# RMSNorm in a hybrid decoder: squares of four channel chunks summed in fp32 before the ones-matmul

## The chip, the cores and the metric

The kernel runs on all 8 cores of one Trainium2 chip, the same program on each (data parallel: one prompt sequence and 16 sample sequences per core). The metric is the device time of the slowest core, in microseconds. Most executions of one kernel agree within 0.3%. In some executions the cores of one die show a lower granted clock and the time is some per cent longer ("slow"); only fast executions are compared here, or, where a chip never was fast, the cores of its undisturbed die (a die is cores 0 to 3, or 4 to 7).

Five engines matter: TensorE (PE, matmuls, writes PSUM), VectorE (DVE), ScalarE (ACT), GpSimd (POOL) and SyncE (SP, DMA). Tiles lie in SBUF, the memory on the chip; the sums of the matmuls lie in PSUM. Each engine executes its own list of instructions in order. Here these lists are fixed when the program is built, by a list scheduler inside the kernel that works with modelled durations.

## The reference, cut to what matters

```python
def _rmsnorm(x, g):
    x32 = x.astype(jnp.float32)
    y = x32 * lax.rsqrt(jnp.mean(x32 * x32, axis=-1, keepdims=True) + RMS_EPS)
    return (y * g.astype(jnp.float32)).astype(x.dtype)

# per layer (2 layers), D_MODEL = 1024
hn = _rmsnorm(x, norm_in);  z = hn @ w_in          # 8 blocks of 1024 columns
...                                                # gated conv, RG-LRU, two output products, merge
x = x + merged @ w_o
gate = sigmoid(_rmsnorm(x, norm_pe) @ w_pg)
x = x + (p @ w_pe) * gate
# at the end: y = _rmsnorm(x, norm_final)
```

There are five norms per token: two per layer and a final one.

## The kernel before

Activations lie feature-major: a token tile of `n` = 424 (or 416) tokens is 8 chunks of 128 channels by `n` tokens. There are 5 token tiles, in two groups, so 25 norms of a tile. The mean over channels crosses partitions, so it is done by TensorE: the square of each chunk is the moving operand against a 128x128 tile that holds 1/1024 ("ones"), and the 8 products accumulate in one PSUM bank.

```python
def norm(t, xs, gcol, prio, final=False, split=(), yield_=0.0):
    n = TN[t]
    hv = [Val("buf", f"hn{t}.{i}") for i in range(KC // 2)]     # bf16 result, two chunks each
    bk = Val("bank", "nps")
    for k in range(KC):                                         # KC = 8 squares, bf16
        ...
        G.op([("act", d_act(n)), ("pool", d_ptt(n)), ("dve", d_stt(n))],   # any of three engines
             fsq, [xs[k]], [(h, p)], prio)
    for k in range(KC):                                         # 8 ones-matmuls
        G.op([("pe", d_mm(n, 1))], lambda e, en, h=h, a=a, k=k: e.matmul(
            out=ps(bk, 0, n), lhsT=ones[:], rhs=b16(h, a, a + n), start=(k == 0), stop=(k == KC - 1)),
            [(h, p), st_ones], [bk], prio, gate=True)
    ...                                                         # rstd = exp(-0.5 ln(mean + eps)) on ScalarE
    for k in range(KC):                                         # hn = x * g * rstd, mostly on VectorE (L570)
        ...
```

`G.op` gives the scheduler the engines that may take an operation, with a modelled duration for each. The scheduler places every operation on the engine that would end it first, by these numbers:

```python
def d_stt(n):  return 0.075 + 1.04e-3 * n    # VectorE tensor_tensor:         0.52 us at 424
def d_sttp(n): return 0.13 + 1.04e-3 * n     # ... with a scalar per partition: 0.57 us
def d_ptt(n):  return 0.3 + 2.4e-3 * n       # GpSimd tensor_tensor:          1.32 us
def d_mm(n, k=8): return k * (n + 6) / 2400. # TensorE, k matmuls:            0.179 us each
```

Two streams of work are interleaved to keep TensorE full: the "A" phase of one token group and the "B" phase of another (output products, merge, `w_o`, second norm, gate). In the A phase a channel block's convolution result is cast to bf16 (L668, ScalarE or VectorE) and goes through two 128x128 gate matmuls (L732, L735).

Of the kernel before, what the change touches and what calls it, by code (L numbers as in the profile page):

```python
# [7 lines left out]
AF = mybir.ActivationFunctionType  # L8
ALU = mybir.AluOpType

D = 1024
KC = 8
# [11 lines left out]
TN = (424, 424, 424, 424, 416)  # L24
T0 = tuple(sum(TN[:i]) for i in range(len(TN)))
GROUPS = ((0, 1), (2, 3, 4))
BUFE = 428
NBUF = 82
RA_N, RA_E = 6, 2048
# [38 lines left out]

class Op:
    __slots__ = ("engs", "fn", "R", "W", "prio", "aset", "dma", "npred", "succ", "ready", "idx", "vals",  # L70
                 "alloc", "eng", "start", "fin", "gate", "stream", "done", "look")


class Graph:
# [17 lines left out]
        self.ops = []  # L92
        self.stream = 0

    def op(self, engs, fn, R, W, prio, aset=None, dma=None, gate=False, after=()):
        o = Op()
        o.engs, o.fn, o.prio, o.aset, o.dma, o.gate = engs, fn, prio, aset, dma, gate
        o.R = [(r if isinstance(r, tuple) else (r, None)) for r in R]
        o.W = [(w if isinstance(w, tuple) else (w, None)) for w in W]
        o.idx = len(self.ops)  # L100
        o.look = self.WIN if dma is None else self.WIN_W if dma[0] in ("d_ra", "d_rb") else 0.0
        if prio < 0:
            o.look = 1e9
        o.stream, o.done = self.stream, False
        o.succ = []
        o.ready = 0.0
        preds = set(after)

        def parts(v, p):
            return (0, 1) if p is None else (p,)  # L110

        for v, p in o.R:
            for q in parts(v, p):
                w = v.lastw.get(q)
                if w is not None:
                    preds.add(w)
                v.readers.setdefault(q, []).append(o)
        for v, p in o.W:
            for q in parts(v, p):
                for r in v.readers.get(q, ()):  # L120
                    if r is not o:
                        preds.add(r)
                w = v.lastw.get(q)
                if w is not None:
                    preds.add(w)
                v.lastw[q] = o
                v.readers[q] = []
        o.vals = {id(v): v for v, _ in o.R + o.W}
        o.alloc = []
        for v in o.vals.values():  # L130
            if v.kind != "static":
                if not v.ops:
                    o.alloc.append(v)
                v.ops.append(o)
        o.npred = len(preds)
        for q in preds:
            q.succ.append(o)
        self.ops.append(o)
        return o

    def schedule(self):
# [55 lines left out]
        while n_left:  # L197
            best = None
            for e in ENG:
                T = free[e]  # L200
                eb = None
                for o in cand[e]:
                    if o.prio < 1e6 and (o.prio > head[o.stream] + o.look or o.prio > head[0] + self.WIN_B):
                        continue
                    a = avail(o) if o.alloc else 0.0
                    if a is None:
                        continue
                    s0 = s = max(T, o.ready + (self.MARGIN if e == "pe" and o.prio > 0 else 0.0), a)
                    key = o.prio
                    if e == "act" and o.aset and not cur[0] & self.SETS[o.aset]:  # L210
                        s = max(T + SW, o.ready, a)
                        key += 30.0
                    if len(o.engs) > 1:

                        d = dict(o.engs)[e]
                        if any(x != e and max(free[x], o.ready, a) + dx < s + d - 0.05 for x, dx in o.engs):
                            continue
                    k2 = (s0 > T + 0.02, s0 if s0 > T + 0.02 else 0.0, key, o.idx)
                    if eb is None or k2 < eb[0]:
                        eb = (k2, s, o)  # L220
                if eb is not None and (best is None or eb[1] < best[0]):
                    best = (eb[1], e, eb[2])
            if best is None:
                stuck = [(e, o.idx, [v.name for v in o.alloc]) for e in ENG for o in cand[e]]
                raise RuntimeError(f"stuck: {stuck[:20]} free {len(bufs['buf'])} {len(bufs['bank'])}")
            s, e, o = best
            dur = dict(o.engs)[e]
            if e == "act" and o.aset:
                cur[0] = (cur[0] & self.SETS[o.aset]) or self.SETS[o.aset]
            for v in o.alloc:  # L230
                if v.kind in ringn:
                    v.phys = v.seq % ringn[v.kind]
                else:
                    fl = bufs[v.kind]
                    x = min(fl)
                    fl.remove(x)
                    v.phys = x[1]
            o.eng, o.start, o.done = e, s, True
            advance(o.stream)
            free[e] = s + dur  # L240
            if o.dma is not None:
                st = max(dma_free[0], s + dur)
                dma_free[0] = st + o.dma[1]
                o.fin = dma_free[0] + (2.4 if e == "pool" else 1.7)
            else:
                o.fin = s + dur + self.LAT[e]["dve"]
            for x, _ in o.engs:
                cand[x].remove(o)
            for q in o.succ:
                q.npred -= 1  # L250
                q.ready = max(q.ready, (s + dur if q.dma is not None and q.dma[0] == o.dma[0] and o.dma[0] in ("d_ra", "d_rb") else o.fin)
                              if o.dma is not None else s + dur + self.LAT[e][q.engs[0][0]])
                if q.npred == 0:
                    for x, _ in q.engs:
                        cand[x].append(q)
            for v in o.vals.values():
                if v.kind == "static":
                    continue
                v.left -= 1
                v.free_at = max(v.free_at, o.fin)  # L260
                if v.left == 0:
                    if v.kind in ringn:
                        ringfree[v.kind][v.seq] = v.free_at
                    else:
                        bufs[v.kind].append((v.free_at, v.phys))
            order.append(o)
            n_left -= 1
# [72 lines left out]
def build_nc():  # L340
# [25 lines left out]
    G = Graph()  # L366
    from contextlib import ExitStack
    with ExitStack() as ctx:
# [16 lines left out]
        ones = sb("ones", [128, 128], BF16)  # L385
# [12 lines left out]
        def f32(v, a, b):  # L398
            return arena[v.phys][:, a:b]

        def b16(v, a, b):
            return arena[v.phys][:].bitcast(BF16)[:, a:b]

        def ps(v, a, b):
            return psum[v.phys][:, a:b]
# [5 lines left out]
        def d_stt(n):  # L411
            return 0.075 + 1.04e-3 * n
# [10 lines left out]
        def d_act(n, ptrs=0):  # L423
            return 0.09 + 0.833e-3 * n + 0.09 * ptrs

        def d_ptt(n):
            return 0.3 + 2.4e-3 * n
# [4 lines left out]
        def d_mm(n, k=8):  # L432
            return k * (n + 6) / 2400.0

        st_vecs, st_dv, st_eps, st_ones = (Val("static", s, s) for s in ("vecs", "dv", "eps", "ones"))
# [91 lines left out]
        def norm(t, xs, gcol, prio, final=False, split=(), yield_=0.0):  # L527

            n = TN[t]
            hv = [Val("buf", f"hn{t}.{i}") for i in range(KC // 2)]  # L530
            bk = Val("bank", "nps")
            for k in range(KC):
                h, p = hv[k // 2], k % 2
                a = p * n
                def fsq(e, en, x=xs[k], h=h, a=a):
                    if en == "act":
                        return e.activation(out=b16(h, a, a + n), in_=f32(x, 0, n), func=AF.Square)  # L537
                    return e.tensor_tensor(out=b16(h, a, a + n), in0=f32(x, 0, n), in1=f32(x, 0, n), op=ALU.mult)  # L538

                G.op([("dve", d_stt(n))] if final and not yield_ and k >= KC - 2 else [("act", d_act(n)), ("pool", d_ptt(n)), ("dve", d_stt(n))],  # L540
                     fsq, [xs[k]], [(h, p)], prio)
            for k in range(KC):
                h, p = hv[k // 2], k % 2
                a = p * n
                G.op([("pe", d_mm(n, 1))], lambda e, en, h=h, a=a, k=k: e.matmul(  # L545
                    out=ps(bk, 0, n), lhsT=ones[:], rhs=b16(h, a, a + n), start=(k == 0), stop=(k == KC - 1)),
                    [(h, p), st_ones], [bk], prio, gate=True)
            rs = Val("buf", f"rstd{t}")
            gx = {}
            for k in split:  # L550
# [7 lines left out]
            for k in range(KC):  # L558
                h, p = hv[k // 2], k % 2
# [553 lines left out]
```

## Time and profile before

| | before |
|---|---|
| time, median of fast runs | 1523.9 us (1523.7 to 1524.7) |
| PE / DVE / ACT / POOL busy, page of the slowest core | 97% / 72% / 69% / 20% |
| matmuls, of them ones-matmuls | 8200, 200 |
| chain that ended last | 93% PE |

From the page (the slowest core of the profiled run, busy us with share of the span), the engine totals, the chain that ended last, and the group of ones-matmuls:

```profile
PE 1499.7 (97%) x8200; PEld 809.8 (53%) x8200; DVE 1105.3 (72%) x1983; ACT 1060.3 (69%) x1574; POOL 306.1 (20%) x655
...
PE 93%; DVE 3%; ACT 2%; DMA 1%; issue 1%; SPq 0%; DVEq 0%; ACTq 0%
...
L545 PE MATMUL ps<-buf,ones 128*128 128x424 bf16 (+1 forms) x200 | 64.8, 354 | 16.0 <-DVE buf L538 7.9
```

TensorE bounds the kernel. A matmul is listed with 0.35 us, but matmuls overlap; the price of one in a full stream is the distance between starts, 0.1785 us on average in the trace of core 4. "TensorE: Matmul & The Clock Gate" in the Trainium skill (section "Back-to-back issue gap") gives N/2.4 + 2.5 ns, which is 179 ns for 424 columns, for what it calls an isolated matmul; the trace has this distance in the stream too.

The windows view of core 4, a core of the faster die (columns: stretch, its length, busy us and number of instructions of PE, PEld, DVE, ACT, POOL, then granted clock, DMA share, GB/s). The first row is an ordinary stretch, the other three lie near norms:

```profile
600.00:620.00 20.00, 20.00 (x114) 11.00 (x113) 9.12 (x16) 12.99 (x17) 1.06 (x2) 1.00 0.55 91
...
480.00:500.00 20.00, 19.67 (x111) 10.47 (x110) 19.89 (x40) 16.70 (x29) 4.27 (x10) 1.00 0.32 66
...
860.00:880.00 20.00, 18.66 (x106) 9.98 (x104) 19.89 (x36) 14.51 (x30) 6.22 (x13) 1.00 0.72 135
...
1220.00:1240.00 20.00, 19.72 (x112) 10.76 (x111) 20.00 (x43) 15.71 (x26) 6.91 (x12) 1.00 0.47 77
```

VectorE's 72% is an average: from 600 to 800 us, far from norms, it has 9 to 13 of 20 us of work, in the stretches near norms shown 19.9 to 20. PE loses little there. The waits view of the same core (total, times, longest):

```profile
PE ps L545 <- DVE buf L538: 8.3, 5, 4.4
...
PE ps L582 <- DVE buf L570: 3.8, 4, 1.9
...
PE ps L732 <- ACT buf L668: 0.8, 2, 0.4
```

The first line belongs to the start and the very end of the run. L570 writes hn; L668 is the cast in front of the gate matmuls.

### The profile page before, as it was taken

What the parts mean: (1) busy time and instruction counts of PE and PEld (TensorE: products, weight loads), DVE (VectorE), ACT (ScalarE), POOL (GpSimd) and SP (SyncE); (2) the same over time, 40 slices, a digit from 0 to 9 for tenths busy, and PEclk for the clock granted to TensorE, in tenths of its full rate; (3) what the DMA queues carried; (4) which work ended last, traced back from release to release, by engine and by line L of the source; (5) the groups of instructions that cost most, each with busy time, mean ns of one, the idle gap of its engine ahead of it and who ended that gap; (6) DMA issues with size and microseconds to landing.
All of it is one profiled execution on the core that took longest, in us unless ns stands there. A gap on an engine that the chain in (4) does not pass through costs nothing.

```text
span 1540.7 us, 23888 instructions; the slowest of 8 cores (1519.4 to 1540.7 us)
## 1 busy us (share of the span) xinstructions
PE 1499.7 (97%) x8200; PEld 809.8 (53%) x8200; DVE 1105.3 (72%) x1983; ACT 1060.3 (69%) x1574; POOL 306.1 (20%) x655
## 2 busy tenths in 40 slices
PE   5999999999999999999999999999999999999995
PEld 2555555555555555555555555555555555555552
DVE  5878878976788986556666968766668897433487
ACT  3999966977779777666567776877767887111364
POOL 3221212221132321101112202222112221010002
PEclk9999999999999999999999999999999999999997
DMA  8777455364464746344766377443474524875303
GB/s 164 122 111 125 117 118 83 55 103 71 117 90 70 140 93 92 63 72 69 147 132 94 63 150 141 68 65 58 67 156 77 81 44 103 189 141 104 53 1 135
DMA packets 66677, 151.99 MB, mean 99 GB/s; under 512 B 7168, under 2 KB 37760, under 8 KB 66560
## 3 DMA queue, kind: packets, MB, share of 16 engines
q0 software_dynamic: 36464, 105.46, 43.7%
q1 hardware_dynamic: 30096, 45.00, 9.5%
q8 instruction: 69, 1.13, 0.3%
q14 instruction: 48, 0.39, 0.1%
HBM read 237.74 MB, written 18.14 MB: 166 GB/s over the span
## 4 chain that ended last, share of the span: by engine, by line
PE 93%; DVE 3%; ACT 2%; DMA 1%; issue 1%; SPq 0%; DVEq 0%; ACTq 0%
PE ps L582 88%; PE ps L545 2%; DVE buf L570 1%; PE ps L732 1%; PE ps L735 1%; PE ps L588 1%; DMA buf<-xin 1%; DVE buf L566 0%; DVE buf L890 0%; ACT L554 0%; DVE buf L657 0%; ACT buf L554 0%; ACT L748 0%; ACT L744 0%; SPq L522 0%
## 5 line engine op out<-in xcount | busy, mean ns | idle before, releaser
L582 PE MATMUL ps<-buf,wa 128*128 128x424 bf16 (+1 forms) x3936 | 755.3, 348 | 1.9 <-DVE buf L570 1.9
L582 PE MATMUL ps<-buf,wb 128*128 128x424 bf16 (+1 forms) x3808 | 710.3, 343 | 2.2 <-DVE buf L570 1.6
L582 PEld LDWEIGHTS ps<-buf,wa 128*128 128x128 bf16 x3936 | 390.8, 99 | 333.5 <-issue 2.3
L582 PEld LDWEIGHTS ps<-buf,wb 128*128 128x128 bf16 x3808 | 373.3, 98 | 314.0 <-issue 5.2
L827 DVE SCALAR_TENSOR_TENSOR buf<-buf,ps 128x424 f32<-128x424 f32 (+1 forms) x160 | 94.2, 592 | 202.2 <-PE ps L582 188.1
L825 ACT ACTIVATE buf<-ps 128x424 f32<-128x424 f32 (+1 forms) x160 | 79.5, 519 | 133.4 <-PE ps L582 133.2
L657 DVE SCALAR_TENSOR_TENSOR buf<-buf,vecs_sb 128x424 f32<-128x424 f32 (+1 forms) x240 | 153.1, 638 | 4.7 <-ACT buf L648 1.5
L537 ACT ACTIVATE buf<-buf 128x424 bf16<-128x424 f32 (+1 forms) x122 | 66.9, 553 | 73.5 <-DVE buf L855 39.7
L570 DVE SCALAR_TENSOR_TENSOR buf<-buf,vecs_sb 128x424 bf16<-128x424 f32 (+1 forms) x154 | 101.3, 728 | 7.8 <-ACT buf L556 7.5
L713 DVE SCALAR_TENSOR_TENSOR buf<-buf,vecs_sb 128x424 f32<-128x424 f32 (+1 forms) x160 | 103.5, 647 | 3.0
L748 ACT ACT_TABLE_LOAD x77 | 98.8, 1283 | 1.4
L744 ACT ACT_TABLE_LOAD x69 | 88.5, 1283 | 1.2
L511 POOL DMA_DIRECT2D wb<-w_M x64 | 35.1, 549 | 231.5 <-PE ps L582 199.1
L545 PE MATMUL ps<-buf,ones 128*128 128x424 bf16 (+1 forms) x200 | 64.8, 354 | 16.0 <-DVE buf L538 7.9
L722 ACT ACT_TABLE_LOAD x55 | 70.6, 1283 | 12.4 <-PE ps L582 11.5
L632 ACT ACTIVATE buf<-ps 128x424 f32<-128x424 f32 (+1 forms) x80 | 40.7, 508 | 54.7 <-PE ps L582 41.9
L752 DVE TENSOR_TENSOR buf<-buf 128x424 f32<-128x424 f32 (+1 forms) x77 | 47.6, 620 | 36.1 <-ACT buf L748 35.8
L855 DVE SCALAR_TENSOR_TENSOR buf<-ps,buf 128x424 f32<-128x424 f32 (+1 forms) x80 | 47.2, 594 | 35.4 <-PE ps L582 33.1
L750 DVE SCALAR_TENSOR_TENSOR buf<-buf 128x424 f32<-128x424 f32 (+1 forms) x80 | 47.6, 595 | 25.8 <-ACT buf L742 25.1
L722 ACT ACTIVATE buf<-ps 128x424 f32<-128x424 f32 (+1 forms) x80 | 41.7, 523 | 35.4 <-PE ps L582 32.8
L682 ACT ACTIVATE buf<-ps 128x424 f32<-128x424 f32 (+1 forms) x80 | 40.9, 512 | 35.1 <-PE ps L582 32.1
L740 ACT ACTIVATE buf<-ps,dv 128x424 f32<-128x424 f32 (+1 forms) x80 | 48.8, 610 | 23.3 <-PE ps L732 23.0
(95 smaller groups left out, 1521.5 us busy)
## 6 DMA issues: line engine op xcount, KB each, us to landing
wa<-w_A POOLq DMA_DIRECT2D x96, 512.0 KB, 10.2
wb<-w_M POOLq DMA_DIRECT2D x64, 512.0 KB, 7.7
buf<-xin SPq DMA_DIRECT2D x64, 212.0 KB, 7.3
wb<-w_G POOLq DMA_DIRECT2D x24, 320.0 KB, 5.7
xsp<-buf SPq DMA_DIRECT2D x32, 212.0 KB, 5.2
buf<-xsp SPq DMA_DIRECT2D x32, 212.0 KB, 7.2
yT<-buf SPq DMA_DIRECT2D x32, 212.0 KB, 2.2
wb<-w_O POOLq DMA_DIRECT2D x24, 256.0 KB, 7.3
```

Of the source, the lines that this page charges most:

```text
L537: return e.activation(out=b16(h, a, a + n), in_=f32(x, 0, n), func=AF.Square)
L545: G.op([("pe", d_mm(n, 1))], lambda e, en, h=h, a=a, k=k: e.matmul(out=ps(bk, 0, n), lhsT=ones[:], rhs=b16(h, a, a + n), start=(k == 0), s ...
L570: G.op([("dve", d_sttp(n))], lambda e, en, x=xs[k], h=h, a=a, k=k: e.scalar_tensor_tensor(out=b16(h, a, a + n), in0=f32(x, 0, n), scalar=v ...
L582: ins = e.matmul(out=ps(bk, 0, n), lhsT=ring[w.phys][:, off + k * 128:off + (k + 1) * 128], rhs=b16(src[k // 2], a, a + n), start=(k == 0) ...
L657: G2(0.1 + 0.01 * d, [("dve", d_sttp(npr))], lambda e, en, d=d: e.scalar_tensor_tensor(out=f32(xc, 0, npr), in0=f32(xb, 3 - d, 3 - d + npr ...
L713: G2(1.3 + 0.01 * d, [("dve", d_sttp(npr))], lambda e, en, d=d: e.scalar_tensor_tensor(out=f32(cv, 0, npr), in0=f32(cu, d, d + npr), scala ...
L722: G2(1.5, [("act", d_act(n))], lambda e, en: e.activation(out=f32(tg, 0, n), in_=ps(bga, 0, n), func=AF.Silu), [bga], [tg], aset="silu")
L740: G2(0.4, [("act", d_act(n, 1))], lambda e, en: e.activation(out=f32(tr, 0, n), in_=ps(bzr, 0, n), func=AF.Tanh, bias=dcol(DV_BRH + lj), s ...
L744: G2(0.5, [("act", d_act(n, 2))], lambda e, en: e.activation(out=f32(av, 0, n), in_=f32(tr, 0, n), func=AF.Exp, bias=dcol(DV_CH + lj), sca ...
L748: G2(0.6, [("act", d_act(n, 1))], lambda e, en: e.activation(out=f32(tr, 0, n), in_=f32(tr, 0, n), func=AF.Sqrt, bias=dcol(DV_QTR), scale= ...
L825: G.op([("act", d_act(n))], lambda e, en, q=q, bm=bm, n=n: e.activation(out=f32(q, 0, n), in_=ps(bm, 0, n), func=AF.Tanh, scale=0.5), [bm] ...
L827: G.op([("dve", d_stt(n))], lambda e, en, q=q, bp=bp, n=n: e.scalar_tensor_tensor(out=f32(q, 0, n), in0=f32(q, 0, n), scalar=1.0, in1=ps(b ...
```

## The change

The intent: TensorE is full, so take work off it. The squares of four chunks are first summed in fp32 (three adds, on GpSimd or VectorE), the sum is rounded to bf16, and two ones-matmuls do what eight did. Norms at the start and the last final norm keep the direct form ("direct"), since their latency is exposed. The ones-matmuls of the new form are planned 2 us after their modelled readiness instead of 0.5 us.

```diff
+SLACK_N = 2.0
+SUM = 4
...
         def norm(t, xs, gcol, prio, final=False, split=(), yield_=0.0):
+            direct = prio < 0 or (final and not yield_)
...
+            if direct:
+                parts = [[k] for k in range(KC)]
+            else:
+                parts = [list(range(k, k + SUM)) for k in range(0, KC, SUM)]
+            for i, ks in enumerate(parts):
...
+                for k in ks:
+                    d = (h, p) if direct else Val("buf", "sq")          # fp32 square
...
+                while len(level) > 1:
+                    for d0, d1 in zip(level[::2], level[1::2]):
+                        top = len(level) == 2
+                        G.op([("pool", d_ptt(n)), ("dve", d_stt(n))], lambda e, en, ...: e.tensor_tensor(
+                            out=b16(h, a, a + n) if top else f32(d0, 0, n), in0=f32(d0, 0, n), in1=f32(d1, 0, n), op=ALU.add),
+                            [d0, d1], [(h, p) if top else d0], prio)
...
-            for k in range(KC):
+            for i in range(len(parts)):
...
-                    [(h, p), st_ones], [bk], prio, gate=True)
+                    [(h, p), st_ones], [bk], prio, gate=True, slack=None if direct else SLACK_N)
```

In the kernel after, lines have moved by 24: L582 is L606, L570 is L594, L668 is L692, L732 is L756. The squares are L551 (ScalarE) and L552, the adds are L561. The scheduler puts 98 adds on VectorE and 34 on GpSimd.

More of the change, by code (lines that the diff above doesn't have):

```diff
@@ L70 @@
     __slots__ = ("engs", "fn", "R", "W", "prio", "aset", "dma", "npred", "succ", "ready", "idx", "vals",
-                 "alloc", "eng", "start", "fin", "gate", "stream", "done", "look")
+                 "alloc", "eng", "start", "fin", "gate", "stream", "done", "look", "slack")
 class Graph:
@@ L93, in __init__, with op @@
         self.stream = 0
-    def op(self, engs, fn, R, W, prio, aset=None, dma=None, gate=False, after=()):
+    def op(self, engs, fn, R, W, prio, aset=None, dma=None, gate=False, after=(), slack=None):
         o = Op()
+        o.slack = (slack if slack is not None else self.MARGIN) if prio > 0 else 0.0
         o.engs, o.fn, o.prio, o.aset, o.dma, o.gate = engs, fn, prio, aset, dma, gate
@@ L207, in schedule @@
                         continue
-                    s0 = s = max(T, o.ready + (self.MARGIN if e == "pe" and o.prio > 0 else 0.0), a)
+                    s0 = s = max(T, o.ready + (o.slack if e == "pe" else 0.0), a)
                     key = o.prio
@@ L529, in norm @@
             n = TN[t]
+            direct = prio < 0 or (final and not yield_)
             hv = [Val("buf", f"hn{t}.{i}") for i in range(KC // 2)]
             bk = Val("bank", "nps")
-            for k in range(KC):
-                h, p = hv[k // 2], k % 2
-                a = p * n
-                def fsq(e, en, x=xs[k], h=h, a=a):
-                    if en == "act":
-                        return e.activation(out=b16(h, a, a + n), in_=f32(x, 0, n), func=AF.Square)
-                    return e.tensor_tensor(out=b16(h, a, a + n), in0=f32(x, 0, n), in1=f32(x, 0, n), op=ALU.mult)
-                G.op([("dve", d_stt(n))] if final and not yield_ and k >= KC - 2 else [("act", d_act(n)), ("pool", d_ptt(n)), ("dve", d_stt(n))],
-                     fsq, [xs[k]], [(h, p)], prio)
@@ L542, in norm, with out, fsq @@
-            for k in range(KC):
-                h, p = hv[k // 2], k % 2
+            if direct:
[3 more added lines that the diff above has]
+            for i, ks in enumerate(parts):
+                h, p = hv[i // 2], i % 2
+                a = p * n
+                level = []
+                for k in ks:
+                    d = (h, p) if direct else Val("buf", "sq")
+                    def out(d=d, a=a):
+                        return b16(d[0], a, a + n) if isinstance(d, tuple) else f32(d, 0, n)
+                    def fsq(e, en, x=xs[k], out=out):
+                        if en == "act":
+                            return e.activation(out=out(), in_=f32(x, 0, n), func=AF.Square)
+                        return e.tensor_tensor(out=out(), in0=f32(x, 0, n), in1=f32(x, 0, n), op=ALU.mult)
+                    G.op([("dve", d_stt(n))] if final and not yield_ and k >= KC - 2 else [("act", d_act(n)), ("pool", d_ptt(n)), ("dve", d_stt(n))],
+                         fsq, [xs[k]], [d], prio)
+                    level.append(d)
+                while len(level) > 1:
+                    up = []
+                    for d0, d1 in zip(level[::2], level[1::2]):
+                        top = len(level) == 2
+                        G.op([("pool", d_ptt(n)), ("dve", d_stt(n))], lambda e, en, d0=d0, d1=d1, top=top, h=h, a=a: e.tensor_tensor(
+                            out=b16(h, a, a + n) if top else f32(d0, 0, n), in0=f32(d0, 0, n), in1=f32(d1, 0, n), op=ALU.add),
+                            [d0, d1], [(h, p) if top else d0], prio)
+                        up.append(d0)
+                    level = up
@@ L544, in norm @@
+            for i in range(len(parts)):
+                h, p = hv[i // 2], i % 2
                 a = p * n
-                G.op([("pe", d_mm(n, 1))], lambda e, en, h=h, a=a, k=k: e.matmul(
-                    out=ps(bk, 0, n), lhsT=ones[:], rhs=b16(h, a, a + n), start=(k == 0), stop=(k == KC - 1)),
-                    [(h, p), st_ones], [bk], prio, gate=True)
+                G.op([("pe", d_mm(n, 1))], lambda e, en, h=h, a=a, i=i: e.matmul(
+                    out=ps(bk, 0, n), lhsT=ones[:], rhs=b16(h, a, a + n), start=(i == 0), stop=(i == len(parts) - 1)),
+                    [(h, p), st_ones], [bk], prio, gate=True, slack=None if direct else SLACK_N)
```

## The prediction

> **What bounds the kernel now.** TensorE. The page gives PE 97% busy, and the chain that ended last is 93% PE (88% the big matmuls, L582). Busy PE time overstates work, because a 128x424 matmul is listed at about 345 ns while the windows view of core 4 counts 114 of them per 20 us: one every 0.176 to 0.179 us. The Trainium skill ("TensorE: Matmul & The Clock Gate", section on the back-to-back issue gap) gives N/2.4 + 2.5 ns, which is 179 ns for 424 columns; the trace agrees (in the timeline eight matmuls plus one ones-matmul take 1.61 us). So the price of a ones-matmul in the stream is 0.179 us, not its listed 0.35 us. On core 4 PE is idle about 13 us before its first full stretch, about 7 us in all between 40 and 1500 us, and it has little to do in the last 18 us.
>
> **What the change removes.** There are 25 norms with 8 ones-matmuls each (200). Three stay as they are (two at the start, the last final norm). The other 22 go from 8 to 2: by the order view 200 become 68, so 132 go. 132 x 0.179 us = 23.6 us. In the windows around the norms (168-236, 464-476, 521-556, 822-860, 886-926, 1188-1216, 1262-1284, 1424-1500 us) PE is busy 315 of 319 us, so nearly all of this sits on the critical path.
>
> **What it adds and moves.** 132 fp32 adds: the order view puts 98 on VectorE and 34 on GpSimd. VectorE costs about 0.60 us each (L830, L752), minus nine squares that leave it: about +50 us, from 72% to about 75% of the span. GpSimd tensor-tensor costs about 1.3 us: about +45 us on an engine at 20%. The Trainium skill ("GPSIMD Engine Reference", section on elementwise cost) calls it about twice as slow as VectorE; the trace agrees (1.3 against 0.6). ScalarE gets about 17 activations more and, going by the order, about eight table loads (1.28 us) fewer: nothing. A norm's chain becomes one to two adds longer (1 to 3 us), mostly hidden: the other stream of matmuls fills PE, and the scheduler places ones-matmuls 2 us after their modelled readiness.
>
> **What is given back.** (a) VectorE is already full near norms: 19.9 and 18.8 of 20 us in 480-520, 19.9 in 860-880, 20.0 and 18.8 in 1220-1260. There PE already waits 0.3 to 1.9 us on L570. More adds there make those waits, or waits of the ones-matmuls on adds, 2 to 4 us longer in sum. (b) The last 35 us: VectorE is 18.2 of 20 busy, and the static order has about three VectorE instructions more there, so the end comes 0 to 2 us later relative to PE, and the removal there (about 2 us) may not be seen. Net gain 23.6 - 5 = about 18.5 us.
>
> **Prediction.** 1505.5 us, range 1497 to 1517 (8 in 10). Faster by over 2%: 0.05. Within 2%: 0.94. Slower by over 2%: 0.01.
>
> **What would show each step right or wrong.** Ones-matmuls 200 to 68, PE instructions 8200 to about 8068; matmuls per 20 us still 114 in full stretches. PE idle outside start and end grows from 7 to 9-12 us, with new waits on the adds or on the VectorE line that writes hn. VectorE busy rises by 40-60 us, GpSimd by 35-50. The time from the last big matmul to the end is unchanged to 2 us longer.
>
> **What would make it wrong.** VectorE being modelled too fast by the scheduler (0.52 us against a real 0.6 to 0.74) could make the ones-matmuls block PE's in-order queue: gain under 8 us. Or GpSimd adds slow VectorE through shared memory ports. Or the freed slots also remove existing waits, and the gain passes 25 us. Or the granted clock differs (0.975 to 0.992 by core here).

## The result, and the profile after

Ratios here are the mean time of one kernel's fast runs over that of the other's fast runs of the same rounds, so not quite the ratio of the medians quoted.

| | before | after |
|---|---|---|
| time, median of fast runs | 1523.9 us | 1529.5 us (1529.1 to 1530.4) |
| ratio | | 1.0037, 95% interval 1.0018 to 1.0057 |
| core compared below | core 4, 1519.4 us, clock 0.992 | core 0, 1527.7 us, clock 0.990 |

The result is right, and the kernel is not faster but 0.4% slower. The profiled execution after was a slow one, with cores 6 and 7 at 1556 us; core 0, with 1527.7 us, is like the cores of fast executions (1525 to 1529) and is used. It is set against core 4 of before.

The page after (slowest core, one of the two slow ones): the matmuls went as planned, but PE's share of the last chain fell from 93% to 67%, and VectorE's rose from 3% to 16%.

```profile
PE 1489.2 (96%) x8068; PEld 797.6 (51%) x8068; DVE 1167.8 (75%) x2062; ACT 1056.2 (68%) x1583; POOL 367.1 (24%) x691
...
PE 67%; DVE 16%; ACT 11%; issue 3%; DMA 1%; POOL 0%; DVEq 0%; SPq 0%; ACTq 0%; POOLq 0%
```

Windows of core 0 (columns as before). The ordinary stretch is as it was; near norms VectorE is full and PE is not:

```profile
600.00:620.00 20.00, 20.00 (x114) 11.00 (x113) 11.49 (x19) 14.07 (x19) 1.24 (x3) 1.00 0.44 75
...
180.00:200.00 20.00, 15.46 (x82) 7.46 (x80) 19.82 (x23) 15.08 (x25) 12.68 (x14) 1.00 0.09 19
...
500.00:520.00 20.00, 17.46 (x97) 9.38 (x96) 19.70 (x38) 14.03 (x25) 11.46 (x17) 1.00 0.52 101
...
880.00:900.00 20.00, 14.85 (x75) 7.53 (x73) 17.26 (x27) 13.84 (x22) 7.15 (x9) 0.91 0.73 119
...
1240.00:1260.00 20.00, 17.56 (x97) 9.36 (x96) 19.56 (x36) 15.31 (x26) 9.95 (x16) 1.00 0.21 36
```

PE's waits on core 0. The gate matmuls (L756) now wait for the cast, which waits for VectorE's convolution; and hn (L594) comes later. The third line is of the start and the very end (1505 to 1514 us), like the L538 line of before:

```profile
PE ps L756 <- ACT buf L692: 14.3, 11, 5.2
PE ps L606 <- DVE buf L594: 9.2, 5, 2.6
PE ps L569 <- DVE buf L552: 9.1, 5, 4.6
```

The difference adds up from the starts of the matmuls in the two traces, between 40 us and the start of the last big matmul:

| term | before, core 4 | after, core 0 | difference |
|---|---|---|---|
| matmul starts in the stretch, at 0.1785 us | 8111 | 7985 | -22.5 us |
| start distances over 0.25 us: what they exceed 0.179 us by, summed | 10.7 us in 24 | 38.2 us in 63 | +27.5 us |
| last big matmul's start to the end | 21.0 us | 24.4 us | +3.4 us |
| sum | | | +8.4 us (measured 8.3) |

So the matmul time was saved in full, and 31 us came back as waits and a later end. Some 3.4 us of the waits' row is a slower clock. The longest wait, 5.15 us at 883 us, left PE at half speed for a while (windows of 2 us; columns: PE busy and matmuls, granted clock, DMA):

```profile
884.00:886.00 2.00, 0.00 (x0) 1.00 1.04 175
...
888.00:890.00 2.00, 1.57 (x5) 0.59 1.09 174
890.00:892.00 2.00, 2.00 (x7) 0.55 1.00 200
892.00:894.00 2.00, 2.00 (x13) 1.00 0.99 169
```

That is the clock gate which "TensorE: Matmul & The Clock Gate" describes (section "What's actually happening": after an idle window the array gets half its clock); the trace agrees, 7 matmuls in 2 us in place of 13.

Why is VectorE late? It has 79 instructions more, some 47 us at 0.60 us. But the timelines show something else. In the kernel before (core 4), the eight instructions that write one hn took 4.66 us:

```profile
191.89 4.66 DVE L570 SCALAR_TENSOR_TENSOR buf<-buf,vecs_sb 128x424 bf16<-128x424 f32 x8 [0.82 <-ACT buf L556]
```

After (core 0), at nearly the same place, the same eight took 8.02 us, while GpSimd did squares and adds beside them:

```profile
191.84 8.02 DVE L594 SCALAR_TENSOR_TENSOR buf<-buf,vecs_sb 128x424 bf16<-128x424 f32 x8
...
189.36 3.31 POOL L552 TENSOR_TENSOR buf<-buf 128x424 f32<-128x424 f32 x3
192.63 4.24 POOL L561 TENSOR_TENSOR buf<-buf 128x424 f32<-128x424 f32 x3
```

Over the 8 cores of the kernel after, I sorted VectorE's 424-column instructions by whether a GpSimd tensor-tensor (of 0.5 us or more) ran beside them for over 90% of their time, or not at all (mean ns, number):

| VectorE instruction | alone | beside a GpSimd tensor-tensor |
|---|---|---|
| scalar-tensor-tensor, SBUF inputs, scalar per partition, bf16 out (writes hn) | 656 (801) | 1385 (63) |
| the same, fp32 out | 653 (2601) | 1384 (32) |
| tensor-tensor, two SBUF inputs, fp32 out | 595 (1064) | 1272 (50) |
| the same, bf16 out | 597 (1624) | 1003 (24) |
| scalar-tensor-tensor, two SBUF inputs, constant scalar, fp32 out | 595 (846) | 590 (37) |
| scalar-tensor-tensor with a PSUM input | 592 (1382) | 581 (68) |
| tensor-tensor with a PSUM input | 593 (984) | 589 (22) |

"GPSIMD Engine Reference" in the Trainium skill (section "Specifications") says that GpSimd's SBUF interfaces are shared with VectorE, with contention for instructions "in a 2-port perf mode or with two SBUF inputs". The trace agrees: about twice the time in three of the rows with two SBUF inputs, no change with a PSUM input.

The 37 of the row that doesn't change show what kind of slowing this is: not half speed, but a wait. For example, L914, which also reads two SBUF inputs, beside an add on GpSimd (core 0):

```profile
883.87 1.47 DVE L914 SCALAR_TENSOR_TENSOR buf<-buf 128x424 f32<-128x424 f32 x1
...
883.53 1.34 POOL L561 TENSOR_TENSOR buf<-buf 128x424 f32<-128x424 f32 x1 [1.14 <-ACT buf L551]
```

The add ends at 884.87, L914 at 885.34 us. Over the 8 cores, 398 of VectorE's 424-column instructions with two SBUF inputs took over 60 ns too long while they overlapped a GpSimd tensor-tensor (of over 0.7 us), and all 398 ended 0.45 to 0.47 us after the end of one. Of the 259 that overlapped one and were not stretched, 25 overlapped only its last 0.20 us, and 234, the 37 among them, ended 0.73 us or more before it did. So in this trace one of the two waits until the other is done: VectorE for GpSimd in the 398, and, it seems, GpSimd for VectorE in the 234. (GpSimd's spans in a profile are rough, so which of them began first can't be read from it.) The chain that leads to PE's longest wait (876 to 890 us) spends half its time in L914.

I call **stretched time** what a VectorE instruction takes over the median of its group (same line, shape, tiles), if it is over 0.1 us, summed over one core. It is 26.6 us before (core 4) and 53.3 us after (core 0). Over all cores after, 24.5 us per core lie beside the GpSimd adds, 9.5 beside its squares, nearly all the rest beside its other tensor-tensors. So an add on GpSimd takes 24.5 / 34 = 0.72 us from VectorE, more than the 0.60 us that VectorE needs to do it.

That is an argument from one trace. Four theories were tried on the chip:

- **A (work):** the VectorE adds as such fill VectorE, and PE waits.
- **B (GpSimd beside VectorE):** GpSimd's tensor-tensors slow VectorE. B1: through the shared way to SBUF. B2: by GpSimd's own slowness (1.4 us per add in the norm's chain, its queue blocked).
- **C (order):** the new static order, the slack or the longer chain is at fault.
- **D (plan):** the order was planned with wrong durations, and VectorE falls behind it.

### The profile page after: what moved, and what is told of

It reads as the page before. It is cut to its first block, busy times and chain, and to the rows that moved or that the text cites. A ratio compares the mean times of both kernels' runs of the same rounds, so it can differ in the third digit from the quotient of the medians.

```text
span 1556.0 us, 23696 instructions; the slowest of 8 cores (1526.0 to 1556.0 us)
## 1 busy us (share of the span) xinstructions
PE 1489.2 (96%) x8068; PEld 797.6 (51%) x8068; DVE 1167.8 (75%) x2062; ACT 1056.2 (68%) x1583; POOL 367.1 (24%) x691
## 4 chain that ended last, share of the span: by engine, by line
PE 67%; DVE 16%; ACT 11%; issue 3%; DMA 1%; POOL 0%; DVEq 0%; SPq 0%; ACTq 0%; POOLq 0%
PE ps L606 65%; DVE buf L594 4%; DVE buf L914 2%; DVE buf L681 2%; DVE buf L912 2%; ACT L746 1%; DVE buf L792 1%; ACT L768 1%; DVE buf L561 1%; ACT L772 1%; PE ps L612 1%; ACT buf L768 1%; PE ps L756 1%; ACT buf L764 1%; PE ps L759 1%
## 5 line engine op out<-in xcount | busy, mean ns | idle before, releaser
L606 PE MATMUL ps<-buf,wa 128*128 128x424 bf16 (+1 forms) x3936 | 745.0, 347 | 2.4 <-DVE buf L594 2.4
L606 PE MATMUL ps<-buf,wb 128*128 128x424 bf16 (+1 forms) x3808 | 718.7, 347 | 9.3 <-DVE buf L594 6.7
L606 PEld LDWEIGHTS ps<-buf,wa 128*128 128x128 bf16 x3936 | 389.4, 99 | 331.4 <-issue 5.0
L606 PEld LDWEIGHTS ps<-buf,wb 128*128 128x128 bf16 x3808 | 376.3, 99 | 329.9 <-issue 17.7
L849 ACT ACTIVATE buf<-ps 128x424 f32<-128x424 f32 (+1 forms) x160 | 80.3, 518 | 133.4 <-PE ps L606 133.1
L681 DVE SCALAR_TENSOR_TENSOR buf<-buf,vecs_sb 128x424 f32<-128x424 f32 (+1 forms) x240 | 156.9, 654 | 4.4 <-ACT buf L672 1.9
L551 ACT ACTIVATE buf<-buf 128x424 f32<-128x424 f32 (+3 forms) x129 | 69.7, 553 | 84.5 <-DVE buf L879 39.6
L594 DVE SCALAR_TENSOR_TENSOR buf<-buf,vecs_sb 128x424 bf16<-128x424 f32 (+1 forms) x154 | 108.6, 746 | 12.9 <-ACT buf L580 10.9
L737 DVE SCALAR_TENSOR_TENSOR buf<-buf,vecs_sb 128x424 f32<-128x424 f32 (+1 forms) x160 | 104.5, 653 | 3.0
L656 ACT ACTIVATE buf<-ps 128x424 f32<-128x424 f32 (+1 forms) x80 | 40.7, 509 | 69.1 <-PE ps L606 56.2
L692 ACT ACTIVATE buf<-buf 128x424 bf16<-128x424 f32 (+1 forms) x63 | 34.8, 552 | 57.3 <-DVE buf L681 47.5
L561 DVE TENSOR_TENSOR buf<-buf 128x424 f32<-128x424 f32 (+3 forms) x98 | 61.3, 629 | 7.0 <-ACT buf L551 5.2
L774 DVE SCALAR_TENSOR_TENSOR buf<-buf 128x424 f32<-128x424 f32 (+1 forms) x80 | 48.5, 606 | 20.6 <-ACT buf L766 20.0
L514 POOL DMA_DIRECT2D wa<-w_A x96 | 52.5, 552 | 37.9 <-PE ps L606 21.4
L748 DVE TENSOR_TENSOR buf<-ps,buf 128x424 f32<-128x424 f32 (+1 forms) x80 | 47.3, 592 | 18.4 <-ACT buf L746 12.9
```

The lines of the kernel that those rows point to most:

```text
L514: fn = lambda e: e.dma_start(out=ring[v.phys][:, 0:cols] if len(src.shape) == 2 else ring[v.phys][:, 0:cols].rearrange("p (j c) -> p j c", ...
L551: return e.activation(out=out(), in_=f32(x, 0, n), func=AF.Square)
L561: G.op([("pool", d_ptt(n)), ("dve", d_stt(n))], lambda e, en, d0=d0, d1=d1, top=top, h=h, a=a: e.tensor_tensor(out=b16(h, a, a + n) if top ...
L594: G.op([("dve", d_sttp(n))], lambda e, en, x=xs[k], h=h, a=a, k=k: e.scalar_tensor_tensor(out=b16(h, a, a + n), in0=f32(x, 0, n), scalar=v ...
L606: ins = e.matmul(out=ps(bk, 0, n), lhsT=ring[w.phys][:, off + k * 128:off + (k + 1) * 128], rhs=b16(src[k // 2], a, a + n), start=(k == 0) ...
L681: G2(0.1 + 0.01 * d, [("dve", d_sttp(npr))], lambda e, en, d=d: e.scalar_tensor_tensor(out=f32(xc, 0, npr), in0=f32(xb, 3 - d, 3 - d + npr ...
```

## The experiments

All times are medians of fast runs. "PE idle" is PE's idle time in the profile between 40 us and its last big matmul; both it and stretched time are of core 0 (before: core 4). The last column counts GpSimd tensor-tensors over 0.7 us.

| run | time us | ratio to before | PE idle us | stretched us | GpSimd |
|---|---|---|---|---|---|
| before | 1523.9 | | 7.0 | 26.6 | 47 |
| after | 1529.5 | 1.0037 | 28.2 | 53.3 | 83 |
| e1 all adds tiny (wrong result) | 1498.2 | 0.9792 | 5.6 | 27.7 | 52 |
| e2 VectorE adds tiny (wrong result) | 1520.5 | 0.9938 | 21.5 | 52.7 | 83 |
| e3 GpSimd adds tiny (wrong result) | 1504.5 | 0.9833 | 9.0 | 28.3 | 53 |
| e4 matmuls put back | 1539.6 | 1.0062 | 19.6 | 51.7 | 83 |
| e5 memset for GpSimd adds (wrong result) | 1506.3 | 0.9878 | 9.1 | 28.3 | 51 |
| e6 same order, adds to VectorE | 1520.9 | 0.9977 | 21.4 | 28.5 | 49 |
| e7 no GpSimd in the norm's sums | 1500.7 | 0.9843 | 8.0 | 16.9 | 25 |
| e8 as e7, bf16 sums | 1501.4 | 0.9847 | 8.7 | 17.0 | 25 |
| e9 before, no GpSimd squares | 1523.7 | 0.9992 | 6.2 | 16.0 | 23 |
| e10 adds on VectorE, squares free | 1513.8 | 0.9928 | 14.1 | 32.4 | 57 |
| e11 adds free, squares not on GpSimd | 1522.1 | 0.9980 | 19.0 | 43.3 | 65 |
| e12 as e7, other tensor-tensors off GpSimd too | 1499.0 | 0.9831 | 5.3 | 10.5 | 13 |
| e13 same order, adds and squares to VectorE | cores 1516 | | 20.6 | 18.8 | 27 |
| e14 / e16 measured VectorE times in the planner | 1512.6 | 0.9920 | 16.5 | 62.7 | 107 |
| e15 as e7, usual slack | cores 1500 | | 6.8 | 17.8 | 25 |
| e17 e7 and e16 together | 1515.2 | 0.9939 | 14.2 | 22.3 | 29 |
| e18 before, measured VectorE times | 1521.6 | 0.9981 | 7.4 | 31.3 | 53 |

(In the rounds of e1 to e4 one run of the kernel before, of 1545.5 us, counted as fast, which widens their intervals and makes their ratios about 0.003 too low; for e1, e3 and e4 the verdict by these ratios is "unclear", but their medians differ from each other by 6 us or more, where their own fast runs lie within 1 us. e13, e14 and e15 fell on a chip whose second die was slow in every run; for e13 and e15 the spans of the undisturbed cores are given, where the kernel before had 1520.)

### The same order, adds made tiny: e1, e2, e3

The order of every engine's list stays as in the kernel after (the traces have the same lists, but for one memset that fills the constant tile at the start); only the width of the adds changes at emission. The summed ones-matmuls read a constant tile, to keep stale data out.

```diff
+  def fadd(e, en, d0=d0, d1=d1, top=top, h=h, a=a):
+      w = 8 if COND else n          # e1: True   e2: en == "dve"   e3: en == "pool"
+      return e.tensor_tensor(out=b16(h, a, a + w) if top else f32(d0, 0, w), in0=f32(d0, 0, w), in1=f32(d1, 0, w), op=ALU.add)
...
-  rhs=b16(h, a, a + n)
+  rhs=b16(h, a, a + n) if direct else flat[:, 0:n]
```

> The changed kernel with its per-engine instruction order kept exactly; only the 132 adds work on 8 columns in place of 424 (and the 44 summed ones-matmuls read a constant tile, so the result is wrong on purpose). Theory A (work: the adds fill VectorE around the norms and TensorE then waits): 1500 to 1506 us, PE idle between 40 and 1500 us back to about 7 us. Theory B (the adds on GpSimd slow VectorE instructions beside them): also 1500 to 1510, since both go. Rival C (the new static order, the 2 us of slack or the longer chain is at fault, not the adds' time): stays at 1520 to 1530.

> As the first run, but only the 98 adds on VectorE shrink, the 34 on GpSimd stay full size. A: nearly all of the loss comes back, 1502 to 1510 us. B: only a part, 1514 to 1524. C: 1520 to 1530.

> As the first run, but only the 34 adds on GpSimd shrink, the 98 on VectorE stay full size. A: little, 1520 to 1527 us. B: most comes back, 1505 to 1514, and the VectorE line that writes hn takes 0.58 us in place of 1.0 us in the stretch where it took 1.0. C: 1520 to 1530.

e1 took 1498.2 us: without the adds' time, the change is worth its 23.6 us and a little more, in the same order (1500 to 1506 had been expected). C falls. e2, without the 98 adds on VectorE, still took 1520.5; e3, without the 34 on GpSimd, took 1504.5, just below the range expected under B. A quarter of the adds, on an engine that is idle three quarters of the time, makes 25 of the 31 us between after and e1; stretched time falls by just as much, 53.3 to 28.3 us. A is the smaller part. (In e3 the instructions that write hn near 192 us take 0.65 to 0.66 us each after the first, as alone; I had expected 0.58.)

The windows of one crowded stretch, after and then e3 (core 0; columns as before):

```profile
830.00:960.00 130.00, 121.98 (x661) 64.79 (x659) 121.37 (x197) 99.55 (x153) 37.85 (x55) 0.97 0.59 117
```

```profile
830.00:960.00 130.00, 128.29 (x713) 69.05 (x712) 119.44 (x215) 103.20 (x162) 33.87 (x66) 1.00 0.58 111
```

VectorE is busy for much the same time in both, but in e3 it gets 215 instructions done in it, and in the kernel after 197.

### The removed matmuls put back: e4

```diff
-  e.matmul(..., lhsT=ones[:], ...)                        # once per sum
+  for r in range(4): e.matmul(..., lhsT=ones4[:], ...)    # ones4 = ones / 4, result unchanged
```

> The changed kernel with its order and its adds, but each sum is fed to TensorE four times with ones/4: the 132 removed matmuls are back and the result is right. If the saved matmul time was realised and the loss is a separate thing, the time is the changed kernel's plus 23 us: about 1550. If VectorE paces the norm stretches (A or B), most of the 132 matmuls fall into TensorE's waits: plus 5 to 15 us, 1533 to 1543.

1539.6 us, 10.1 more than after: 132 matmuls worth 23.6 us cost 10. More than half of what the change takes from TensorE is hidden in waits, as expected when VectorE paces these stretches.

### GpSimd busy, but not reading: e5

```diff
+  if o.mv and o.eng == "pool":                           # o.mv: one of the adds
+      P.op("pool", lambda e: e.memset(scrp[:], 0.0), R, [("scrp", 0)])
   P.op(o.eng, ...)                                       # the tiny add of e3
```

> The changed kernel's order; each of the 34 adds on GpSimd is replaced by a memset of about 1.25 us that reads nothing, then an add of 8 columns (wrong result on purpose). GpSimd stays as long in the norm's chain and in its own queue as with the add. B1 (a GpSimd add slows VectorE instructions that read two SBUF tensors, by sharing their way to memory): 1503 to 1510 us, as in the run with small GpSimd adds (1504.6), and VectorE's stretched time stays near 28 us as there. B2 (it is GpSimd's own 1.4 us in the norm's chain and in its in-order queue): 1520 to 1530 us.

1506.3 us. GpSimd is kept as long as by an add, in the same place of its queue and of the norm's chain (the group view of e5, GpSimd; busy us, mean ns, idle before):

```profile
L1000 POOL MEMSET scrp<- 128x1360 bf16 x34 | 41.8, 1231 | 46.0 <-ACT buf L556 40.0 <-DVE buf L557 5.8
```

Yet the loss is gone, and stretched time is 28.3 us as in e3. Beside the memset, the instructions that write hn took 653 ns (64 of them), as alone. So it is not GpSimd's slowness in the chain, nor its queue, which also holds the issues of weight transfers (B2), but its reading and adding beside VectorE (B1).

### Adds on VectorE: e6, e7, e8

e6 keeps the order and moves the 34 adds to VectorE after scheduling:

```diff
   order = G.schedule()
+  for o in order:
+      if o.mv:
+          o.eng = "dve"
```

e7 takes GpSimd out of the choices before scheduling. e8 also keeps squares and sums in bf16:

```diff
-  [("act", d_act(n)), ("pool", d_ptt(n)), ("dve", d_stt(n))]    # squares
+  [("act", d_act(n)), ("dve", d_stt(n))]
-  G.op([("pool", d_ptt(n)), ("dve", d_stt(n))], ...             # adds
+  G.op([("dve", d_stt(n))], ...                                 # e8: bf16 tiles, and d_ts(n)
```

> The changed kernel, scheduled as it is; after scheduling, the 34 adds that stand on GpSimd are given to VectorE at the same place in the order (result right). VectorE gets about 20 us more work and loses about 25 us of stretching. B1: 1504 to 1513 us. B2: also below 1515, since the chain is shorter. A (the amount of VectorE work): 1528 or more.

> The changed kernel with GpSimd taken out of the norm's squares and adds before scheduling (squares on ScalarE or VectorE, adds on VectorE, result right). B1: 1500 to 1510 us, stretched VectorE time 15 to 22 us. A: 1528 or more.

> As the run before, and squares and partial sums are bf16 tiles, so that a VectorE add should take about 0.32 us in place of 0.60 us (estimate: the fp32 TENSOR_SCALAR of the same size[...] takes 0.45 to 0.50 us, so 0.3 to 0.5). Result right within tolerance. If VectorE paces the norm stretches: 1496 to 1503 us, below the fp32 version by 3 to 8 us. If it no longer does: the same as the run before.

e7 took 1500.7 us (two fast runs), a right result, 1.6% under before: the whole predicted matmul saving, with all 132 adds on VectorE. Its stretch at 830 us, where VectorE now does 230 instructions:

```profile
830.00:960.00 130.00, 128.11 (x715) 69.44 (x714) 124.97 (x230) 103.45 (x160) 31.84 (x54) 1.00 0.55 110
```

e8 is the same as e7, though a bf16 add takes 0.376 us in place of 0.598: once GpSimd is out of the way and the plan knows it, VectorE no longer paces.

e6 missed my expectation (1504 to 1513): 1520.9 us, with stretched time gone as hoped (28.5 us). The same adds on VectorE cost 16 us in this order (e3: 1504.5) and nothing in e7's. So B1 is not all of it. The expectation counted the stretching that goes but not enough of the work that comes: on core 0 VectorE is busy 1166 us in the kernel after, 1158 us in e6 and 1141 us in e3 and e5. At these places of the order VectorE's time is short, whatever takes it.

### Which GpSimd work, and what of the kernel before: e9, e10, e11, e12

The edits are those of e7 in parts: e9 the squares' line in the kernel before; e10 the adds' line; e11 the squares' line; e12 all `("pool", ...)` choices beside `("dve", ...)`, the other products of the A and B phase too.

> The kernel before (eight ones-matmuls, no adds), only GpSimd is taken from the engines that may do the squares. If the gain of the run without GpSimd in the norm (0.984) comes from fewer matmuls, this one stays within 5 us of the kernel before: 1519 to 1526. If it comes from freeing VectorE of GpSimd's squares alone, it falls to 1505 or below.

> The changed kernel with adds on VectorE alone before scheduling; squares may go to GpSimd, and the order view shows that 35 do (24 in the changed kernel). If a GpSimd tensor-tensor beside the norm costs, whatever it computes (B1): 1508 to 1522 us, stretched VectorE time 30 us or more. If only the adds on GpSimd cost: 1500 to 1505.

> The changed kernel with squares never on GpSimd; adds may go there, and the order view shows that 39 do (34 in the changed kernel). B1: 1512 to 1528 us, stretched VectorE time 35 us or more. If only squares on GpSimd cost: 1500 to 1505.

> The run without GpSimd in the norm's squares and adds, and in addition every other tensor-tensor that may choose between GpSimd and VectorE goes to VectorE; on GpSimd 12 are left. B1 allows a little more: 1496 to 1501 us, stretched VectorE time 8 to 14 us. If VectorE's sheer work now limits: 1502 to 1510.

In the changed kernel, re-planned each time: GpSimd in both 1529.5, in the squares alone 1513.8, in the adds alone 1522.1, in neither 1500.7. Either kind of tensor-tensor costs. In the kernel before, the same removal is worth nothing (1523.7 against 1524.8 in the same rounds), though stretched time falls there by 11 us: before the change VectorE had room. e12 is the fastest right version, 1499.0 us, ratio 0.983 (interval 0.982 to 0.985).

### The order and the planner: e13 to e18

e13 moves adds and squares to VectorE in the fixed order (as e6, with `o.mv` set on the squares too). e14, and e16 again, tell the planner what VectorE really takes:

```diff
-  def d_stt(n):  return 0.075 + 1.04e-3 * n
-  def d_sttp(n): return 0.13 + 1.04e-3 * n
+  def d_stt(n):  return 0.155 + 1.04e-3 * n     # 0.60 us at 424, as measured
+  def d_sttp(n): return 0.21 + 1.04e-3 * n      # 0.65 us
```

e15 is e7 with `slack=None` for the ones-matmuls, e17 is e7 with e14's numbers, e18 is the kernel before with them.

> The changed kernel's order; after scheduling, the 34 adds and the 24 squares on GpSimd all go to VectorE in place (result right). If the squares left on GpSimd kept the earlier run at 1521: 1503 to 1512 us. If the fixed order is the cause (the work was planned to run beside VectorE, so VectorE is too full at those places): 1520 to 1535 us, stretched VectorE time 17 to 20 us.

> The changed kernel; the planner is told 0.60 and 0.65 us for VectorE's tensor-tensor and scalar-tensor-tensor instructions (measured), in place of 0.52 and 0.57. It then gives GpSimd more: by the order view 54 adds, 24 squares and 17 others in place of 34, 24 and 13. If the planner's error in VectorE's times is the cause: 1500 to 1515 us. If GpSimd beside VectorE is (B1): 1525 to 1545 us, stretched VectorE time 60 us or more.

> The run without GpSimd in the norm, with the ones-matmuls planned with the usual slack of 0.5 us in place of 2 us. If the slack matters: 1505 to 1515 us with waits of the ones-matmuls on adds; if not: 1499 to 1504 us.

> The changed kernel with measured VectorE times in the planner, once more: 1509 to 1514 us in the fast state, 13 to 20 us under the changed kernel, though it has more GpSimd tensor-tensors and more stretched VectorE time (63 us) than that. If the earlier reading came of the slow chip: 1525 or more.

> No GpSimd in the norm and measured VectorE times in the planner. If the two cures mend the same lateness of VectorE, the second adds little: 1497 to 1502 us. If they are separate losses: 1490 or below.

> The kernel before with measured VectorE times in the planner. PE there waits only 7 us between 40 and 1500 us, so 1518 to 1526 us. If the planner's times were a loss in both kernels: 1510 or below.

- e13: 1516 us on undisturbed cores (after: 1527; e7: 1496 to 1499), stretched time 18.8 us. With hardly any contention left, PE is idle for 20.6 us in this order: VectorE now does the 58 instructions that were planned to run beside it. The time lies between the two ranges expected (1503 to 1512, 1520 to 1535), nearer to that of the fixed order.
- e14: 1507 to 1511 us on undisturbed cores, which is what was expected if the planner's times are at fault (1500 to 1515), and not if B1 is (1525 or more); e16, in the fast state, 1512.6, so it was not the chip. It has more GpSimd adds (54) and more stretched time (62.7 us) than after, and is 17 us faster. So stretched time does not by itself cost time. That the planner, with true VectorE times, leaves room into which the stretching falls is the likely reading; no run shows it.
- e15: 1498 to 1503 on undisturbed cores. In e7's plan the slack has no part; in the plan of the kernel after, e1 keeps the slack and has no loss.
- e18: 1521.6, 3 us under before. The planner's numbers matter little while VectorE has room.
- e17: 1515.2, where I expected 1502 or, if separate, 1490. Here PE waits mostly for ScalarE, as the waits view of its core 0 shows (5.8 us of the first line are of the start; the two L606 lines make 8 of the 14 us of PE idle):

```profile
PE ps L569 <- ACT buf L551: 8.6, 8, 5.8
...
PE ps L606 <- ACT buf L764: 4.6, 3, 4.1
...
PE ps L606 <- ACT buf L746: 3.5, 3, 1.7
```

That plan is bad at another engine. It says that two re-plannings of one kernel can differ by 15 us, so a difference between re-planned kernels is weaker evidence than e1 to e6, which share one order. That e7, e8, e12 and e15, four different plans, all lie at 1499 to 1501 us speaks for e7 not being a lucky one.

**What is shown.** The loss is VectorE falling behind a fixed order in the stretches around the norms, with PE's in-order list waiting behind it. In that order, the GpSimd adds are the larger cause, because VectorE's two-SBUF-input instructions wait for them (e3, e5); the VectorE adds are the smaller one (e2). Both act because that order has no room for VectorE at those places (e6, e13; e16, another plan, is in line with it). **What stays open:** which places of e16's plan absorb its stretched time, why e17's plan overloads ScalarE, and what decides which of VectorE and GpSimd waits.

## Why the prediction was wrong, point by point

- *TensorE bounds, a ones-matmul costs 0.179 us, 132 of them 23.6 us:* right. 200 became 68, PE's count 8068, the start distance stayed 0.1785 us, and e7 gains 23 us against the kernel before.
- *Nearly all of it lies on the critical path:* true of the old plan, and no longer of the new one. With the matmuls put back the time rose by only 10 us (e4).
- *VectorE +50 us, GpSimd +45 us "on an engine at 20%":* **this is the step that failed.** The GpSimd adds were costed on GpSimd alone, as if VectorE ran on undisturbed. Measured by the pages: VectorE +62.5 us, GpSimd +61 us. Each GpSimd add took 0.72 us from VectorE, and with these adds made tiny 25 of the 31 us between after and e1 came back (e3). Where GpSimd is busy as long but leaves VectorE alone, which is what the prediction assumed, the kernel takes 1506.3 us with 9.1 us of PE idle (e5), against the predicted 1505.5 us and 9 to 12 us: the rest of the sum held. The text named this contention only among what could make it wrong, though the L570 instructions beside GpSimd were already at 1.47 us in the trace of before (48 over its cores).
- *Waits 2 to 4 us longer near norms:* the place was largely right (480-520, 860-880, 1220-1260 us), the size was not: start distances in excess grew by 27.5 us. PE idle grew from 7 to 28 us, not to 9-12. The prediction had read rightly that VectorE was full there (19.9 to 20 of 20 us); what it left out is the VectorE time that the GpSimd adds take at these places.
- *The end 0 to 2 us later:* 3.4 us.
- *ScalarE: nothing:* right, 1060 to 1056 us.
- *The planner's short VectorE times as a risk:* right as a risk. e16, planned with measured times, is 17 us faster than after, but e17 is 15 us slower with them than e7, so its size is not shown.
- *Clock:* named as a difference between cores only. Two of the new waits (at 861 and 888 us) were followed by 3.4 us each at half the clock, which is 3.4 us of time in all.
- The time, 1529.5, lies above the range (1497 to 1517); "within 2%" held.

## What to carry to other kernels

An idle GpSimd is not free room beside a busy VectorE: here a tensor-tensor given to it took more VectorE time (0.72 us) than VectorE needs to do it (0.60 us), unless VectorE was reading PSUM or had slack. One of the two waited until the other was done. Before moving work off the bottleneck onto "72% busy" engines, read their windows where the work will land, and if the order is fixed at build time, give the planner measured durations and then time its plan (with them e16 was 17 us faster than after, e17 15 us slower than e7). To find such a cause, keep the order fixed and shrink one engine's share of the new work at a time, then replace it by something equally long that doesn't read.

## What the Trainium skill lacked or had wrong

- "GPSIMD Engine Reference": it names the contention of VectorE instructions with two SBUF inputs, but not its size. (This is about that page alone; I don't claim that no other page tells more.) Here: 656 to 1385 ns and 595 to 1272 ns for 424 columns beside a GpSimd tensor-tensor, 581 to 592 ns with a PSUM input either way. A stretched one ended 0.45 to 0.47 us after the GpSimd instruction (398 of 398).
- "GPSIMD Engine Reference" (section on engine selection) advises VectorE for element-wise work because GpSimd is about twice as slow; the cost to VectorE itself, 0.72 us per GpSimd add here, is not in that page's reason.
- "TensorE: Matmul & The Clock Gate", section "Back-to-back issue gap": N/2.4 + 2.5 ns is said to hold for an isolated matmul and to over-count in a stream at large N. In this stream of 424-column matmuls, each with its own weight load, it is just the distance, 178.5 ns over some 8000.
- The same page, section "What's actually happening": an idle window of about 3.4 us brings the half clock. Here a wait of 2.64 us (at 861 us, core 0, after) was followed by the half clock, too, 0.50 from 862 to 864 us; waits of 2.0 to 2.2 us (200, 480 and 1218 us) were not.
